# The crossbar's merges two steps later, A21-A22 taken before the transposes, contiguous merge writes

## The chip, the cores and the metric

The kernel runs on one core of one Trainium2 chip. The metric is device time in microseconds, the median of several executions. The engines are PE (matrix products, with PEld for its weight loads), DVE (vector), ACT (scalar: copies and activation functions), POOL (here it issues the accumulating DMAs) and SP (here it issues most of the DMAs). Each engine works through its own queue in order, and waits where an operand is not ready.

## What is computed

A trunk of two layers on x of 512 tokens by 1024 features. Each layer adds half a SwiGLU network, a token mixer, and half a second SwiGLU network; the first layer's mixer is a gated linear recurrence, the second's a spatial gating unit over chunks of 128 tokens. The part that the change touches is the SwiGLU network, which occurs four times with a hidden width of 2816:

```
def swiglu(x, w_in, w_out):
    g, u = jnp.split(x @ w_in, 2, axis=-1)
    return (jax.nn.silu(g) * u) @ w_out

for i in range(DEPTH):
    h = h + 0.5 * swiglu(rms_norm(h, ffn1_norm[i]), ffn1_w_in[i], ffn1_w_out[i])
    ...
    h = h + 0.5 * swiglu(rms_norm(h, ffn2_norm[i]), ffn2_w_in[i], ffn2_w_out[i])
return rms_norm(h, final_norm)
```

Everything is fp32 in and out.

## The kernel before

**Products.** An fp32 factor is split into a high part (`hi`, `whi`: a rounded copy, made by ACT) and a low part (`lo`, `wlo`: the difference, made by DVE), and a product is three matmuls, hi x hi, hi x lo and lo x hi (L423 to L425). On top of that, products of large blocks go by a scheme with seven products in place of eight of a 2 x 2 block product (`seven`). Its left factors are A11, A12, A22 and the sums S1 = A21 - A22, S2 = S1 - A11, S4 = S2 + A12, S3 = -S2 - A22; here A11 and A12 are the left and right half of the features for the first 256 tokens, A21 and A22 those of the last 256 tokens. The products are called P1, P2, P5, P6, P3, P7 and Q4, in this order, on A11, A12, S1, S2, S4, S3 and A22 (`ORDER`, `LEFT`). The right factors are blocks of weights, loaded by SP into buffers `raw`, some of them added to on the way by POOL's accumulating DMAs, some added by DVE (`raw<-raw,raw`).

**One SwiGLU network** (`ffn`) goes through the hidden width in three parts: a pair of 128-column tiles and a chunk of four, then twice a chunk of four and a chunk of four. Each part makes the hidden tiles of its two pieces (`pair_plain` or `chunk`), and then multiplies them by their rows of the output weights (`out_blocks`). In a chunk the products go to PSUM banks A, B and C, ACT and DVE copy and combine them into SBUF tiles `c`, and the gated hidden tiles come out after P3 (tokens 0 to 255, half 0) and after Q4 (tokens 256 to 511, half 1).

**Transposing the hidden tiles.** The output product needs them with features on partitions. For the second piece of each part PE transposes them (L268, tile `e`), one step after they are made. For the first piece (`whole=True`; the pair in one part of three, a chunk of four in the others) it is done by the DMA crossbar, which moves 16-bit elements: `Group.cross` has ACT separate the high and low 16 bits of each fp32 element into planes (`pl`), SP issue the crossbar transposes of the planes (`dt`), and ACT merge the two transposed planes into fp32 again (`merge`). There are twelve such first pieces, each with two halves and two merges to a half. Then `parts` splits a block into hi and lo, and `sums` makes S2, S4 and S3 on DVE.

**Order.** All instructions stand in an order written out by hand. The program runs through a list of steps; a step is one weight block of one product (12 matmuls in a chunk), and a chunk has 14 steps. At step i the loop (L1629 on) runs the hooks `pre`, splits the weights up to step i + 3, runs the hooks `mid` and `rest`, issues loads into buffers that came free, then issues the step's matmuls, and runs the hooks `end` and `late`. `hook(n, phase, fn)` puts work at step n. In `cross` at step n, before: planes at n `mid`, transposes at n `rest`, the two merges at n + 3 and n + 4 (L328), the parts of A11 and A12 at n + 5 and n + 6 (L330), or for half 1 S1's subtraction and its parts at n + 5 (L332, L333), and S2, S4 and S3 from n + 6 (L763). The call follows a chunk's P3 or Q4 by one step, a pair's by two. Small tiles come from a pool of 60 slots.

Of the kernel before, what the change touches and what calls it, by code (L numbers as in the profile page):

```python
# [10 lines left out]
U16 = mybir.dt.uint16  # L11
AF = mybir.ActivationFunctionType
ALU = mybir.AluOpType

P = 128
D = 1024
T = 512
# [36 lines left out]
def trunk(ctx: ExitStack, tc: tile.TileContext, a: dict, out: bass.AP):  # L54
    nc = tc.nc
    PS = bass.MemoryType.PSUM
    cp = ctx.enter_context(tc.tile_pool(name="cp", bufs=1))
    sp = ctx.enter_context(tc.tile_pool(name="sp", bufs=SLOTS))
# [9 lines left out]
    def nm(s):  # L68
        uid[0] += 1
        return f"{s}_{uid[0]}"  # L70
# [16 lines left out]
    def tt(o, x, y, op):  # L87
        nc.vector.tensor_tensor(out=o, in0=x, in1=y, op=op)  # L88
# [7 lines left out]
    def act(o, x, f, **k):  # L96
        nc.scalar.activation(out=o, in_=x, func=f, **k)  # L97
# [118 lines left out]
    def hook(n, phase, fn):  # L216


        hooks.setdefault((n, phase), []).append(fn)
# [29 lines left out]
    class Group:  # L249
# [45 lines left out]
            for c, g in cs:  # L295
                stt(lo[:, c], ps[:, c], g, f32(hi[:, c]), ALU.mult, ALU.subtract)

        def cross(self, n, names, tiles):

            w, pl, dt = 4 * self.n * P, [], {}  # L300

            def planes():
                for h in tiles:
                    t = sp.tile([P, 2 * T], U16, tag="s", name=nm("pl"))[:, :w]
                    act(t.rearrange("p (k b f) -> p k b f", k=2, b=2),
                        h.bitcast(U16).rearrange("p (k f b) -> p k b f", k=2, b=2), AF.Copy)
                    pl.append(t)
                tiles.clear()

            def move():  # L310
                for name, k in names:
                    d = dt[name] = sp.tile([P, 2 * T], U16, tag="s", name=nm("dt"))[:, :w]
                    v = d.rearrange("p (m s t) -> p m s t", s=2, t=P)
                    for s, t in enumerate(pl):
                        nc.sync.dma_start_transpose(out=v[:, :, s, :], in_=t[:, k * w // 2 : (k + 1) * w // 2])
                pl.clear()

            def merge(name):
                t = self.new("S1" if name == "A21" else name)
                act(t.bitcast(U16).rearrange("p (x b) -> p b x", b=2), dt.pop(name).rearrange("p (b x) -> p b x", b=2), AF.Copy)  # L320

            def s1():
                tt(self.f["S1"], self.f["S1"], self.f["A22"], ALU.subtract)
# [12 lines left out]

# [467 lines left out]
    def chunk(w_in, f0, nt, group, opening=None, whole=False):  # L804
# [47 lines left out]
    def pair_plain(w_in, f0, group, first=False):  # L852
# [819 lines left out]
```

## Time and profile before

| | |
|---|---|
| time, median of 3 runs | 1595.22 us (1595.11 to 1600.31) |
| the profiled execution's own time | 1601.47 us |
| its span, first to last instruction | 1599.8 us |
| granted clock of TensorE, mean | 0.999 |
| crossbar transposes (SP) | 96, 3.8 us from issue to landing (median; 2.3 to 8.4) |
| merges (ACT) | 48: 32 of 128x1024 and 16 of 128x512 16-bit elements |
| plane copies (ACT) | 48: 32 of 128x1024 and 16 of 128x512 |
| DMA moved | 289.79 MB, mean 181 GB/s |

How to read the rows: a row of waits names an engine, what it was to write and the helper's line, then who ended the wait, the total in us, the times, and the longest. A row of a timeline has the start in us, the duration in us, the engine, line, operation, what it writes `<-` what it reads, the shapes, and in brackets the idle time of the engine just before it and what ended that. L97, L88 and L94 are the helpers through which all ACT and DVE work goes, so that the tile names tell what an instruction is. A row of a group by shape ends with the count, the busy time in us and the mean duration in ns, and the idle time before them.

### The profile page before, as it was taken

To read this page: it belongs to the slowest core of one execution; us is meant where nothing else is said; L and a number is where in the kernel's file an instruction comes from. 1 tells how busy PE (TensorE), PEld (TensorE's weight loads), DVE (VectorE), ACT (ScalarE), POOL (GpSimd) and SP (SyncE) were. 2 spreads that over 40 slices of the span, in tenths; PEclk is the share of its full clock that TensorE was granted. 3 is DMA by queue.
4 is the path that set the end of the run, shared out by engine and by line. 5 is a ranking of instruction groups with operands and counts; after the bars stand their busy time and mean duration, and the time that the engine had idled before them with its cause. 6 is when DMAs were issued, how large, how long until landed. Compare 5 with 4: busy or idle time off the path is not lost.

```text
span 1599.8 us, 20767 instructions
## 1 busy us (share of the span) xinstructions
PE 1585.2 (99%) x7293; PEld 1314.5 (82%) x7293; DVE 1368.5 (86%) x1834; ACT 1098.4 (69%) x1567; POOL 223.1 (14%) x201
## 2 busy tenths in 40 slices
PE   9999999999999999999999999999999999999998
PEld 7778888898888888888788888888888888888886
DVE  6898897888998897877888978878978988889788
ACT  7757657668777657557677576576886875675676
POOL 2111111100010111111102111111211011111120
PEclk9999999999999999999999999999999999999999
DMA  8779978853294788978838788778878657796793
GB/s 287 175 170 185 226 168 193 213 150 103 82 215 104 175 189 196 220 173 174 213 112 185 177 192 213 178 179 215 226 196 207 158 127 196 179 221 173 173 223 104
DMA packets 208297, 289.79 MB, mean 181 GB/s; under 512 B 55505, under 2 KB 81217, under 8 KB 208193
## 3 DMA queue, kind: packets, MB, share of 16 engines
q1 hardware_dynamic: 158688, 195.33, 40.0%
q0 software_dynamic: 47712, 91.30, 34.4%
q10 hardware_dynamic: 1792, 1.84, 0.4%
q8 instruction: 57, 0.93, 0.2%
q14 instruction: 48, 0.39, 0.1%
HBM read 275.84 MB, written 2.10 MB: 174 GB/s over the span
## 4 chain that ended last, share of the span: by engine, by line
PE 90%; DMA 4%; DVE 3%; issue 1%; ACT 1%; SPq 0%; POOL 0%; ACTq 0%; DVEq 0%; POOLq 0%
PE A L425 13%; PE A L424 13%; PE A L423 13%; PE C L424 7%; PE C L425 7%; PE C L423 7%; PE p L870 4%; PE B L425 4%; PE B L424 4%; PE B L423 4%; PE e L268 2%; PE r L226 2%; PE r L228 2%; PE r L227 2%; DMA raw<-in_ffn_w_in_dram 2%; DMA dt<-pl 1%
## 5 line engine op out<-in xcount | busy, mean ns | idle before, releaser
L88 DVE TENSOR_TENSOR wlo<-raw,whi 128x1024 fp32r<-128x1024 f32 (+1 forms) x537 | 639.2, 1194 | 170.9 <-ACT whi L97 164.6
L97 ACT ACTIVATE whi<-raw 128x1024 fp32r<-128x1024 f32 (+1 forms) x537 | 553.7, 1034 | 324.6 <-PE A L424 81.1
L423 PE MATMUL A<-whi,hi 128*128 128x512 f32 x1016 | 399.0, 393 | 0.8 <-ACT c L97 0.8
L425 PE MATMUL A<-wlo,hi 128*128 128x512 f32 x1016 | 396.0, 390 | 0.0
L424 PE MATMUL A<-whi,lo 128*128 128x512 f32 x1016 | 395.8, 390 | 0.0
L425 PEld LDWEIGHTS A<-wlo,hi 128*128 128x128 f32 x1016 | 190.7, 188 | 40.1 <-DVE wlo L88 0.4
L423 PEld LDWEIGHTS A<-whi,hi 128*128 128x128 f32 x1016 | 190.9, 188 | 39.6 <-ACT c L97 1.2
L424 PEld LDWEIGHTS A<-whi,lo 128*128 128x128 f32 x1016 | 190.9, 188 | 38.8 <-DVE lo L88 0.3
L424 PE MATMUL C<-whi,lo 128*128 128x512 f32 x560 | 218.8, 391 | 1.2 <-DVE lo L88 1.2
L423 PE MATMUL C<-whi,hi 128*128 128x512 f32 x560 | 219.1, 391 | 0.7 <-ACT hi L97 0.7
L425 PE MATMUL C<-wlo,hi 128*128 128x512 f32 x560 | 218.7, 390 | 0.0
L139 POOL DMA_DIRECT2D raw<-in_ffn_w_in_dram x82 | 99.1, 1216 | 718.2 <-DMA raw<-in_ffn_w_out_dram 302.6
L139 POOL DMA_DIRECT2D raw<-in_ffn_w_out_dram x72 | 83.3, 1196 | 376.5 <-DVE wlo L88 152.4
L88 DVE TENSOR_TENSOR raw<-raw,raw 128x1024 f32<-128x1024 f32 x108 | 129.8, 1202 | 0.5
L88 DVE TENSOR_TENSOR lo<-a,hi 128x512 fp32r<-128x512 f32 (+1 forms) x188 | 123.0, 662 | 2.9 <-ACT hi L97 2.8
L424 PEld LDWEIGHTS C<-whi,lo 128*128 128x128 f32 x560 | 105.5, 188 | 23.9 <-DVE lo L88 2.0
L97 ACT ACTIVATE hi<-a 128x512 fp32r<-128x512 f32 (+1 forms) x188 | 111.9, 600 | 18.8 <-DVE a L88 16.6
L423 PEld LDWEIGHTS C<-whi,hi 128*128 128x128 f32 x560 | 105.4, 188 | 23.1 <-ACT hi L97 1.1
L425 PEld LDWEIGHTS C<-wlo,hi 128*128 128x128 f32 x560 | 105.6, 188 | 21.9
L424 PE MATMUL B<-whi,lo 128*128 128x512 f32 x280 | 109.1, 390 | 0.1
L423 PE MATMUL B<-whi,hi 128*128 128x512 f32 x280 | 109.1, 390 | 0.0
L425 PE MATMUL B<-wlo,hi 128*128 128x512 f32 x280 | 109.0, 389 | 0.0
(183 smaller groups left out, 2102.7 us busy)
## 6 DMA issues: line engine op xcount, KB each, us to landing
raw<-in_ffn_w_in_dram SPq DMA_DIRECT2D x161, 512.0 KB, 4.5
raw<-in_ffn_w_out_dram SPq DMA_DIRECT2D x100, 512.0 KB, 5.0
raw<-in_ffn_w_in_dram POOLq DMA_DIRECT2D x82, 512.0 KB, 6.7
raw<-in_ffn_w_out_dram POOLq DMA_DIRECT2D x60, 512.0 KB, 7.8
raw<-in_sg_w_in_dram SPq DMA_DIRECT2D x20, 512.0 KB, 6.7
raw<-in_ffn_w_in_dram SPq DMA_DIRECT2D x34, 256.0 KB, 5.1
raw<-in_rec_w_in_dram SPq DMA_DIRECT2D x16, 512.0 KB, 3.9
raw<-in_sg_w_in_dram POOLq DMA_DIRECT2D x12, 512.0 KB, 8.4
```

The costliest lines, as they stand in the source:

```text
L88: nc.vector.tensor_tensor(out=o, in0=x, in1=y, op=op)
L97: nc.scalar.activation(out=o, in_=x, func=f, **k)
L139: nc.gpsimd.dma_start(out=self.v, in_=src, accum_op=ALU.add)
L226: nc.tensor.matmul(ps, wh, xh, start=start, stop=False)
L227: nc.tensor.matmul(ps, wh, xl, start=False, stop=False)
L228: nc.tensor.matmul(ps, wl, xh, start=False, stop=stop)
L268: nc.tensor.transpose(ps[:, o : o + P], src(q, s), ident)
L423: nc.tensor.matmul(ps, zh, wh, start=fresh and i == 0, stop=False, **k)
L424: nc.tensor.matmul(ps, zl, wh, start=False, stop=False, **k)
L425: nc.tensor.matmul(ps, zh, wl, start=False, stop=end, **k)
L870: nc.tensor.matmul(bank_of(half, s), z, (sub.lo if m == 2 else sub.hi)[:, q, :], start=left[2] == "2" and (h, q, m) == (0, 0, 0), stop=lef ...
```

## The change

**Timing.** The merges go from steps n + 3 and n + 4 to n + 5 and n + 6, the parts of the left blocks from n + 5 and n + 6 to n + 7 and n + 8, and S2, S4 and S3 from n + 6, n + 7 and n + 8 to n + 8, n + 9 and n + 10.

**A21 - A22.** Before, A22 and A21 were transposed, A21 was merged into S1's tile, and DVE subtracted A22 from it. Now DVE subtracts the right half from the left half of each token tile of half 1, in place, before the planes are made; the left half that goes through the crossbar is S1 itself. One subtraction per half 1 is replaced by two of half the width.

**Planes and merges.** The planes are copied by halves of the features, four copies in place of two for each half of the tokens, each followed by its transpose. The merge runs over the elements with the two planes as its inner loop: it writes contiguously and reads from the two planes in turn. Before it ran over one plane after the other, reading contiguously and writing every second 16-bit element.

```
-            hook(n, "mid", planes)
-            hook(n, "rest", move)
-            for i, (name, _) in enumerate(names):
-                hook(n + 3 + i, "mid", lambda name=name: merge(name))
-                if name in ("A11", "A12"):
-                    hook(n + 5 + i, "mid", lambda name=name: self.parts(name))
-            if names[-1][0] == "A21":
-                hook(n + 5, "pre", s1)
-                hook(n + 5, "mid", lambda: self.parts("S1"))
+            def move():
+                pl = [sp.tile([P, 2 * T], U16, tag="s", name=nm("pl"))[:, : 2 * w] for _ in tiles]
+                for k, name in enumerate(names):
+                    c = slice(k * w, (k + 1) * w)
+                    d = dt[name] = sp.tile([P, 2 * T], U16, tag="s", name=nm("dt"))[:, : 2 * w]
+                    v = d.rearrange("p (m s t) -> p m s t", s=2, t=P)
+                    for s, (t, h) in enumerate(zip(pl, tiles)):
+                        act(t[:, c].rearrange("p (b f) -> p b f", b=2),
+                            h.bitcast(U16)[:, c].rearrange("p (f b) -> p b f", b=2), AF.Copy)
+                        nc.sync.dma_start_transpose(out=v[:, :, s, :], in_=t[:, c])
                 tiles.clear()
...
             def merge(name):
-                t = self.new("S1" if name == "A21" else name)
-                act(t.bitcast(U16).rearrange("p (x b) -> p b x", b=2), dt.pop(name).rearrange("p (b x) -> p b x", b=2), AF.Copy)
+                act(self.new(name).bitcast(U16).rearrange("p (x b) -> p x b", b=2),
+                    dt.pop(name).rearrange("p (b x) -> p x b", b=2), AF.Copy)
...
         if whole:
-            g.cross(n, (("A22", 1), ("A21", 0)) if half else (("A11", 0), ("A12", 1)),
-                    [tiles.pop(2 * half + s) for s in range(2)])
+            hs = [tiles[2 * half + s] for s in range(2)]
             if half:
-                sums(g, n + 6)
+                for h in hs:
+                    tt(h[:, : g.n * P], h[:, : g.n * P], h[:, g.n * P :], ALU.subtract)
+                sums(g, n + 8)
+            g.cross(half, hs, (n, "mid"), ((n + 5, "mid"), (n + 6, "mid")), [(n + 7, "mid"), (n + 8, "mid")][: 2 - half])
             return
```

The instructions of PE, SP and POOL and their order stay as they were, but for names and which half of the features a transpose carries first. What moves stands on ACT and DVE.

ACT in the third part of the first layer's second network (near 740 us), where the first chunk's blocks are merged while the second chunk is multiplied. Before:

```order
L97 ACTIVATE whi_6803<-raw_6450 128x1024
L97 ACTIVATE hi_6807<-a_1446_6748 128x512
L97 ACTIVATE whi_6826<-raw_6428 128x1024
L97 ACTIVATE a_1468_6831<-dt_6754 128x2x512
L97 ACTIVATE whi_6847<-raw_6450 128x1024
L97 ACTIVATE s_1471_6852<-dt_6757 128x2x512
L97 ACTIVATE c_1458_6792<-c_1458_6792,rt_4669 128x512
L97 ACTIVATE c_1459_6800<-c_1459_6800,rt_4669 128x512
L97 ACTIVATE whi_6871<-raw_6632 128x1024
L97 ACTIVATE hi_6875<-s_1471_6852 128x512
```

The same place on ACT, after:

```order
L97 ACTIVATE a_1459_6832<-dt_6686 128x1024
L97 ACTIVATE whi_6849<-raw_6453 128x1024
L97 ACTIVATE hi_6854<-a_1454_6809 128x512
L97 ACTIVATE whi_6872<-raw_6475 128x1024
L97 ACTIVATE hi_6877<-a_1459_6832 128x512
L97 ACTIVATE c_1455_6817<-c_1455_6817,rt_4684 128x512
L97 ACTIVATE c_1456_6825<-c_1456_6825,rt_4684 128x512
L97 ACTIVATE whi_6897<-raw_6657 128x1024
L97 ACTIVATE s_1474_6901<-dt_6777 128x1024
L97 ACTIVATE c_1476_6911<-C_6883 128x512
L97 ACTIVATE c_1477_6919<-C_6884 128x512
L97 ACTIVATE whi_6921<-raw_6691 128x1024
```

The merges of half 1 (A22 and S1 before, S1 first after) have moved behind two more weight splits, and where they stood there are now the hi parts of A11 and A12.

DVE at the same place, up to the gating of the second chunk (`c<-c,rt,c`), whose tiles PE then transposes. Before:

```order
L88 TENSOR_TENSOR wlo_6848<-raw_6450,whi_6847 128x1024
L88 TENSOR_TENSOR s_1471_6852<-s_1471_6852,a_1468_6831 128x512
L88 TENSOR_TENSOR wlo_6872<-raw_6632,whi_6871 128x1024
L88 TENSOR_TENSOR lo_6876<-s_1471_6852,hi_6875 128x512
L88 TENSOR_TENSOR a_1440_6720<-s_1471_6852,a_1440_6720 128x512
L88 TENSOR_TENSOR wlo_6899<-raw_6664,whi_6898 128x1024
L88 TENSOR_TENSOR a_1446_6748<-a_1440_6720,a_1446_6748 128x512
L88 TENSOR_TENSOR wlo_6918<-raw_6592,whi_6917 128x1024
L94 SCALAR_TENSOR_TENSOR s_1471_6852<-a_1440_6720,a_1468_6831 128x512
L88 TENSOR_TENSOR wlo_6941<-raw_6614,whi_6940 128x1024
L88 TENSOR_TENSOR wlo_6960<-raw_6428,whi_6959 128x1024
L88 TENSOR_TENSOR c_1487_6929<-C_6856,c_1487_6929 128x512
```

The same place on DVE, after:

```order
L88 TENSOR_TENSOR wlo_6922<-raw_6691,whi_6921 128x1024
L88 TENSOR_TENSOR wlo_6942<-raw_6617,whi_6941 128x1024
L88 TENSOR_TENSOR lo_6946<-s_1474_6901,hi_6945 128x512
L88 TENSOR_TENSOR a_1454_6809<-s_1474_6901,a_1454_6809 128x512
L88 TENSOR_TENSOR wlo_6969<-raw_6639,whi_6968 128x1024
L88 TENSOR_TENSOR a_1459_6832<-a_1454_6809,a_1459_6832 128x512
L88 TENSOR_TENSOR wlo_6989<-raw_6453,whi_6988 128x1024
L88 TENSOR_TENSOR c_1487_6957<-C_6883,c_1487_6957 128x512
L94 SCALAR_TENSOR_TENSOR c_1487_6957<-c_1487_6957,rt_4684,c_1455_6817 128x512
L88 TENSOR_TENSOR c_1488_6965<-C_6884,c_1488_6965 128x512
L94 SCALAR_TENSOR_TENSOR c_1488_6965<-c_1488_6965,rt_4684,c_1456_6825 128x512
L94 SCALAR_TENSOR_TENSOR s_1474_6901<-a_1454_6809,a_1480_6925 128x512
```

S1's subtraction is gone, S1's lo part and the sums S2 and S4 (`a<-s,a`, `a<-a,a`) stand two weight splits nearer to the gating, and S3 (`s<-a,a`) behind it.

ACT in the opening (near 58 us), where the pair's half 0 is merged and the copies `c<-A` free bank A for PE. Before:

```order
L97 ACTIVATE whi_637<-raw_279 128x1024
L97 ACTIVATE hi_641<-s_89_427 128x512
L97 ACTIVATE a_143_645<-dt_536 128x2x256
L97 ACTIVATE pl_647<-h_588 128x512
L97 ACTIVATE pl_649<-h_592 128x512
L97 ACTIVATE c_149_665<-A_161 128x512
L97 ACTIVATE c_150_673<-A_162 128x512
L97 ACTIVATE whi_675<-raw_307 128x1024
L97 ACTIVATE hi_679<-a_137_621 128x256
```

The same place on ACT, after:

```order
L97 ACTIVATE whi_639<-raw_279 128x1024
L97 ACTIVATE hi_643<-s_89_427 128x512
L97 ACTIVATE pl_647<-h_590 128x256
L97 ACTIVATE pl_648<-h_594 128x256
L97 ACTIVATE pl_647<-h_590 128x256
L97 ACTIVATE pl_648<-h_594 128x256
L97 ACTIVATE c_147_667<-A_161 128x512
L97 ACTIVATE c_148_675<-A_162 128x512
L97 ACTIVATE whi_677<-raw_307 128x1024
L97 ACTIVATE a_151_681<-dt_531 128x512
L97 ACTIVATE whi_698<-raw_159 128x1024
L97 ACTIVATE a_155_702<-dt_536 128x512
```

The merge that stood ahead of the plane copies and of the copies from bank A has moved behind them.

More of the change, by code (lines that the diff above doesn't have):

```diff
@@ L296, in direct @@
                 stt(lo[:, c], ps[:, c], g, f32(hi[:, c]), ALU.mult, ALU.subtract)
[L298 to L307, printed above, removed]
-                tiles.clear()
[L310 to L316, printed above, removed]
-            def merge(name):
-                t = self.new("S1" if name == "A21" else name)
-                act(t.bitcast(U16).rearrange("p (x b) -> p b x", b=2), dt.pop(name).rearrange("p (b x) -> p b x", b=2), AF.Copy)
-            def s1():
-                tt(self.f["S1"], self.f["S1"], self.f["A22"], ALU.subtract)
-            hook(n, "mid", planes)
-            hook(n, "rest", move)
-            for i, (name, _) in enumerate(names):
-                hook(n + 3 + i, "mid", lambda name=name: merge(name))
-                if name in ("A11", "A12"):
-                    hook(n + 5 + i, "mid", lambda name=name: self.parts(name))
-            if names[-1][0] == "A21":
-                hook(n + 5, "pre", s1)
-                hook(n + 5, "mid", lambda: self.parts("S1"))
@@ new lines, in cross @@
+        def cross(self, half, tiles, planes, merges, parts):
+            w, names = 2 * self.n * P, ("A12", "A11") if half == 0 else ("S1", "A22")
+            if half == 0:
+                names = names[::-1]
+            dt = {}
+            def move():
[8 more added lines that the diff above has]
+                        nc.sync.dma_start_transpose(out=v[:, :, s, :], in_=t[:, c])
+                tiles.clear()
+            def merge(name):
+                act(self.new(name).bitcast(U16).rearrange("p (x b) -> p x b", b=2),
+                    dt.pop(name).rearrange("p (b x) -> p x b", b=2), AF.Copy)
+            hook(*planes, move)
+            for name, at in zip(names, merges):
+                hook(*at, lambda name=name: merge(name))
+            for name, at in zip(names, parts):
+                hook(*at, lambda name=name: self.parts(name))
```

## The prediction

> **What bounds the kernel now.** I read the page's busy shares first, then the waits of PE by stretches, then ACT's waits on the crossbar, and last the rows around single PE waits.
>
> ```profile
> PE 1585.2 (99%) x7293; PEld 1314.5 (82%) x7293; DVE 1368.5 (86%) x1834; ACT 1098.4 (69%) x1567; POOL 223.1 (14%) x201
> ```
>
> PE is busy in all but 14.6 us of the 1599.8 us span. The change leaves PE's instructions and their order alone, so it wins or loses only in PE's waits. Of the next rows the first four are the waits of PE between 40 and 92 us (the opening), the last is all of them after 92 us:
>
> ```profile
> PE e L268 <- DVE c L94: 1.5, 3, 1.1
> PE C L424 <- DVE lo L88: 1.2, 1, 1.2
> PE A L423 <- ACT c L97: 0.8, 1, 0.8
> PE C L423 <- ACT hi L97: 0.7, 1, 0.7
> ...
> PE e L268 <- DVE c L94: 2.5, 5, 1.0
> ```
>
> One such wait in PE's timeline:
>
> ```profile
> 289.35 0.39 PE L423 MATMUL A<-whi,hi 128*128 128x512 f32 x1
> 289.57 0.39 PE L424 MATMUL A<-whi,lo 128*128 128x512 f32 x1
> ...
> 292.07 0.27 PE L268 MATMUL e<-ident,c 128*128 128x128 f32 x1
> 292.84 0.98 PE L268 MATMUL e<-ident,c 128*128 128x128 f32 x7 [0.50 <-DVE c L94]
> ```
>
> Matmuls start 0.22 to 0.23 us apart but are drawn 0.39 long, so each recorded wait costs about 0.16 us more than it shows. After 92 us that makes 2.5 + 5 x 0.16 = 3.3 us. In the opening it is 1.0 us for bank A, 1.5 + 0.5 = 2.0 us for the transposes, and 1.9 + 0.3 = 2.2 us for bank C at the first output block, where the clock then falls:
>
> ```profile
> 85.00:90.00 5.00, 4.10 (x11) 0.66 0.35 61
> ```
>
> The columns are PE's busy time and matmuls, the granted clock, and DMA. A third of the clock for 5 us is 1.7 us. All that this change could touch is thus 3.3 + 1.0 + 2.0 + 2.2 + 1.7 = 10.2 us.
>
> Where these waits come from. ACT waits for the crossbar's transposes 13 times, 24.6 us in all:
>
> ```profile
> ACT a L97 <- DMA dt<-pl: 20.4, 9, 3.6
> ACT s L97 <- DMA dt<-pl: 4.2, 4, 1.9
> ```
>
> The place with the longest PE wait after 92 us, ACT and then DVE:
>
> ```profile
> 744.16 1.37 ACT L97 ACTIVATE a<-dt 128x1024 uint16<-128x1024 uint16 x1 [3.43 <-DMA dt<-pl]
> 747.74 1.36 ACT L97 ACTIVATE s<-dt 128x1024 uint16<-128x1024 uint16 x1 [1.31 <-DMA dt<-pl]
> ...
> 746.46 1.23 DVE L88 TENSOR_TENSOR wlo<-raw,whi 128x1024 fp32r<-128x1024 f32 x1 [1.68 <-ACT whi L97]
> 749.14 0.70 DVE L88 TENSOR_TENSOR s<-s,a 128x512 f32<-128x512 f32 x1 [1.45 <-ACT s L97]
> 751.27 1.23 DVE L88 TENSOR_TENSOR wlo<-raw,whi 128x1024 fp32r<-128x1024 f32 x1 [1.44 <-PE A L425]
> ...
> 756.58 0.68 DVE L94 SCALAR_TENSOR_TENSOR s<-a,a 128x512 f32<-128x512 f32 x1
> 757.18 2.35 DVE L88 TENSOR_TENSOR wlo<-raw,whi 128x1024 fp32r<-128x1024 f32 x2
> 759.45 0.69 DVE L88 TENSOR_TENSOR c<-C,c 128x512 f32<-128x512 f32 x1
> ...
> 761.56 0.75 DVE L94 SCALAR_TENSOR_TENSOR c<-c,rt,c 128x512 f32<-128x512 f32 x1
> 762.37 0.99 PE L268 MATMUL e<-ident,c 128*128 128x128 f32 x7 [1.00 <-DVE c L94]
> ```
>
> Two merges hold ACT 3.43 + 1.31 = 4.7 us, the weight splits behind them come late, DVE stands idle 1.68 + 1.45 + 1.44 = 4.6 us, then runs without a gap from 751.27 to 762.3 and hands the gated tile c to PE's transposes late. The opening, in the same order of cause:
>
> ```profile
> 57.74 0.79 ACT L97 ACTIVATE a<-dt 128x512 uint16<-128x512 uint16 x1 [1.52 <-DMA dt<-pl]
> 60.05 0.50 PE L423 MATMUL A<-whi,hi 128*128 128x512 f32 x1 [0.82 <-ACT c L97]
> 61.47 1.23 DVE L88 TENSOR_TENSOR wlo<-raw,whi 128x1024 fp32r<-128x1024 f32 x1 [3.60 <-ACT whi L97]
> 67.33 0.98 PE L268 MATMUL e<-ident,c 128*128 128x128 f32 x7 [1.06 <-DVE c L94]
> 79.39 1.06 ACT L97 ACTIVATE whi<-raw 128x1024 fp32r<-128x1024 f32 x1 [4.14 <-DMA raw<-in_ffn_w_out_dram]
> ```
>
> The merge at 57.74 delays the plane copies, the copies that free bank A, and through whi the DVE. The row at 79.39 is another matter: there a weight block is late.
>
> **The change part by part.** Prices of one instruction, from the groups by shape (busy in total, mean ns):
>
> ```profile
> L97 ACT ACTIVATE a<-dt 128x1024 uint16<-128x1024 uint16 x24 | 32.9, 1372 | 19.0 <-DMA dt<-pl 18.8
> L97 ACT ACTIVATE pl<-c 128x1024 uint16<-128x1024 uint16 x32 | 32.9, 1054 | 2.7 <-DVE c L94 2.6
> L97 ACT ACTIVATE a<-dt 128x512 uint16<-128x512 uint16 x12 | 9.3, 777 | 1.5 <-DMA dt<-pl 1.5
> L97 ACT ACTIVATE pl<-h 128x512 uint16<-128x512 uint16 x16 | 9.0, 612 | 0.0
> L88 DVE TENSOR_TENSOR a<-y,h 128x256 f32<-128x256 f32 x16 | 5.8, 422 | 0.0
> L88 DVE TENSOR_TENSOR s<-s,a 128x512 f32<-128x512 f32 x8 | 5.5, 693 | 5.3 <-ACT s L97 5.2
> ```
>
> *Merges two steps later.* A chunk's step is 12 matmuls, 12 x 0.227 = 2.7 us, so each merge gets 5.4 us more; the longest wait is 3.6 us. All 13 waits should go. At the place above ACT is free 4.7 us earlier, against a PE wait of 1.25 + 0.32 = 1.6 us. What is late next there: DVE's work before c. It loses S1's subtraction and the sum s<-a,a (0.69 us each, the latter now behind c), and the halves' lo parts move two steps towards c but stay inside DVE's former idle time. I let all 3.3 us after 92 us go. In the opening the 1.52 us wait goes against PE's 1.0 us for bank A, and DVE's 3.60 us against 1.5 of the 2.0 us of transposes: 2.5 us. The wait for bank C and the clock stay, because the weight block at 79.39 is bound by its transfer: 0.
>
> *Parts and sums behind them.* In the opening the sum a<-a,a of 128x256 now stands before s<-e,a, which feeds bank C's wait. That is one 0.42 us at most, and I count it in full: +0.4 us. Elsewhere the sums S4 and S3 are needed only in the output block, after the rest of the second chunk.
>
> *A21-A22 on token tiles.* Twelve subtractions leave DVE (8 of 0.69, 4 of about 0.42 us). There come 16 of 128x256 (0.42 each) and 8 of 128x128, which no row shows: between half of 0.42 and 0.42. Together DVE changes by -7.2 + 6.8 + 1.7 to 3.4, at most +3 us over twelve places. They stand right behind the last gating of a chunk, and the plane copies on ACT, the transposes on SP, the weight loads behind these on SP, and PE through whi now wait up to 0.84 us longer there. The merge that stood ahead of the plane copies (1.37 us) has moved away, which pays for that: 0.
>
> *Planes by half, merges written contiguously.* 64 copies of 128x512 and 32 of 128x256 replace 32 and 16 of twice the size. By busy time (9.0 / 16 = 0.56 against 32.9 / 32 = 1.03) a pair costs 0.1 us more per large copy, and the small ones lie between 0.28 and 0.56 each: +3 to +12 us on ACT in all. A merge that reads both planes in turn is in no row. Below stands the plane copy, which also writes contiguously (1054 ns); above I take twice the present merge (2744 ns), since each element may be fetched alone. I take the near one, 1054: 32 x 0.32 + 16 x 0.165 = -12.9 us on ACT. ACT is busy 69%, so 0.8 us of each step are free, and this is worth 0 on the path.
>
> [...] The rows say that stepping by two elements on the write side (1372) costs more than on the read side (1054). [...]
>
> *Queues.* SP's and POOL's instructions keep their order; only the transposes of half 1 carry the left half first. 96 transposes as before: 0.
>
> **The sum.** -3.3 - 2.5 + 0.4 = -5.4 us against the profiled execution, 1601.5 to 1596.1. The median of the runs, 1595.2, is 6.3 us below the profiled one, and some of that may be these very waits being shorter. If all of it came out of the 10.2 us in proportion, 0.38 x 5.4 = 2.1 us are left to gain; if none, 5.4. I take the middle, 3.7: 1591.5 us.
>
> **The rivals.**
> - *The opening loosens too.* Everything up to the second plane copies runs 2.5 us earlier, so the weight loads behind the transposes on SP do as well, bank C's wait (2.2) and the clock's fall (1.7) go. For it: the loads stand behind the transposes. Against it: PE arrives earlier by the same 2.5 us. All 10.2 us then: about 1585.
> - *Nothing to gain.* The change does not do what it says: in the median runs the transposes land in time and the merges hardly wait, or the sums and lo parts moved towards c fill DVE as its idle time did. For it: the 6.3 us between profile and median. Then 1594 to 1597.
> - *Slower: the merge that reads in turn.* If it takes t instead of 1.37 us, two merges in two successive steps have 1.37 + 0.84 = 2.2 us each before ACT runs over; there it decides. At 2.7 us each of the 32 large ones overruns by 0.5: 17 us at most, 11 us if the three-step lead of the splits swallows a third, some 1606. Against it: the plane copy's steps cost nothing visible. [...]
>
> **How the numbers follow.** First case 0.65, with its own range 1589.5 to 1594; the opening loosens 0.06; nothing to gain 0.18; slow merges 0.11, of which 0.03 stay within the bound. A measurement of this kernel tells about 0.5% from no change, 8 us: below 1587.2 is faster, above 1603.2 slower. Faster is the loosened opening and a tail of the first case, 0.07; slower 0.08; the rest, 0.85, lies between. The range from 1586.5 to 1600 leaves out most of the loosened opening and of the slow merges, 0.14 together, and holds the 1600.3 us that one run of the kernel before took.
>
> **What would show it.** Right: ACT's waits on dt<-pl at most 2 us in all; PE's waits on c after 92 us under 0.8 us; bank A's wait near 60 us gone; merges of 128x1024 near 1.05 us. Wrong: merges over 2.2 us with DVE waiting for whi behind them; new waits of PE on whi or wlo in the second chunk; DVE without a gap before c as now; bank C's wait grown by more than 0.4 us.

## The result and the profile after

| | before | after |
|---|---|---|
| median of 12 runs each | 1597.82 us (1595.11 to 1602.51) | 1596.55 us (1594.33 to 1597.82) |
| ratio after / before | | 0.9990, 95% interval 0.9981 to 0.9999 |
| the profiled execution's own time | 1601.47 us | 1596.20 us |
| its span | 1599.8 us | 1594.5 us |

The time is 1.3 us lower, less than a measurement of this kernel tells from no change by the prediction's bound of 0.5%. Between the two profiled executions the difference is 5.3 us, close to the 5.4 of the forecast sum, but what makes it up is different, and most of it does not show in the medians. By the starts of the same matmuls in the two traces, about 3.7 us are gained in the opening and 3.6 us later, and 2.0 us are lost.

The busy shares, after:

```profile
PE 1584.9 (99%) x7293; PEld 1313.9 (82%) x7293; DVE 1370.3 (86%) x1846; ACT 1099.0 (69%) x1615; POOL 222.2 (14%) x201
```

PE is as busy as before; what can differ is its waits and its granted clock. All of PE's waits from 40 us to the end, after (the products' lines L423 to L425 are L415 to L417 now):

```profile
PE C L416 <- DVE lo L88: 1.2, 1, 1.2
PE C L415 <- ACT hi L97: 0.5, 1, 0.5
```

The waits for the gated tile `c` and the one for bank A near 60 us are gone. On ACT no wait for a transpose (`dt<-pl`) is left of the 24.6 us. Bank C's wait at the first output block is still there, and so is the fall of the clock behind it. The windows of the opening, after (PE busy and matmuls, PEld, DVE, ACT, POOL, granted clock, DMA share, GB/s):

```profile
80.00:85.00 5.00, 3.28 (x10) 2.38 (x10) 5.00 (x9) 3.14 (x5) 0.00 (x0) 0.82 0.50 110
85.00:90.00 5.00, 5.00 (x20) 4.07 (x19) 5.00 (x11) 2.52 (x4) 2.10 (x2) 0.84 0.50 86
```

The groups by shape, after (count, busy us, mean ns, idle before):

```profile
L97 ACT ACTIVATE pl<-c 128x512 uint16<-128x512 uint16 x64 | 36.0, 622 | 7.7 <-DVE c L94 6.0 <-DVE c L88 1.7
...
L97 ACT ACTIVATE a<-dt 128x1024 uint16<-128x1024 uint16 x24 | 28.1, 1172 | 0.0
L97 ACT ACTIVATE pl<-h 128x256 uint16<-128x256 uint16 x32 | 10.6, 403 | 0.0
...
L88 DVE TENSOR_TENSOR h<-h 128x128 f32<-128x128 f32 x8 | 1.9, 282 | 0.0
```

A merge of 128x1024 takes 1172 ns in place of 1372, and the subtraction of 128x128, which no row of before shows, 282 ns. The plane copies now wait for DVE 7.7 us in all, where it was 2.7.

One new wait stands in no list of waits, because it is hardly longer than the 0.16 us by which a matmul is drawn too long; it shows in the starts. ACT and then PE near 136 us, where a chunk of four is about to go through the crossbar, after:

```profile
131.31 1.06 ACT L97 ACTIVATE whi<-raw 128x1024 fp32r<-128x1024 f32 x1 [1.66 <-PE C L416]
132.40 0.63 ACT L97 ACTIVATE pl<-c 128x512 uint16<-128x512 uint16 x1
133.79 1.68 ACT L97 ACTIVATE pl<-c 128x512 uint16<-128x512 uint16 x3 [0.76 <-DVE c L94]
...
136.32 1.26 ACT L97 ACTIVATE c<-A 128x512 f32<-128x512 f32 x2
...
136.32 0.39 PE L416 MATMUL A<-whi,lo 128*128 128x512 f32 x1
136.55 0.39 PE L417 MATMUL A<-wlo,hi 128*128 128x512 f32 x1
136.95 0.50 PE L415 MATMUL A<-whi,hi 128*128 128x512 f32 x1
137.28 0.40 PE L416 MATMUL A<-whi,lo 128*128 128x512 f32 x1
```

The same place on ACT, before:

```profile
134.97 1.06 ACT L97 ACTIVATE whi<-raw 128x1024 fp32r<-128x1024 f32 x1 [1.66 <-PE C L424]
136.07 1.06 ACT L97 ACTIVATE pl<-c 128x1024 uint16<-128x1024 uint16 x1
137.45 1.06 ACT L97 ACTIVATE pl<-c 128x1024 uint16<-128x1024 uint16 x1 [0.33 <-DVE c L94]
...
139.37 0.58 ACT L97 ACTIVATE c<-A 128x512 f32<-128x512 f32 x1
```

Read from the `whi` in the first row of each, the copy that frees bank A starts 5.01 us later in the kernel after (136.32 - 131.31) and 4.40 us later in the kernel before (139.37 - 134.97), a difference of 0.6 us. With copies by halves the first is the left half of token tile 0, the second already needs token tile 1, which DVE finishes later, so ACT waits 0.76 us with half of tile 0 uncopied. PE's matmuls, 0.227 us apart elsewhere, start 0.40 and 0.33 us apart here. That is 0.3 us at this place, about 0.2 us at the mean of eight (near 137, 253, 604, 721, 931, 1047, 1387 and 1504 us), and 1.7 us in all.

### The profile page after: what moved, and what is told of

It is laid out like the page before. It is cut to its first block, busy times and chain, and to the rows that moved or that the text cites. A ratio compares the mean times of both kernels' runs of the same rounds, so it can differ in the third digit from the quotient of the medians.

```text
span 1594.5 us, 20905 instructions
## 1 busy us (share of the span) xinstructions
PE 1584.9 (99%) x7293; PEld 1313.9 (82%) x7293; DVE 1370.3 (86%) x1846; ACT 1099.0 (69%) x1615; POOL 222.2 (14%) x201
## 4 chain that ended last, share of the span: by engine, by line
PE 94%; DMA 3%; DVE 1%; issue 0%; ACT 0%; SPq 0%; POOL 0%; POOLq 0%; ACTq 0%; DVEq 0%
PE A L415 14%; PE A L416 14%; PE A L417 14%; PE C L416 8%; PE C L417 8%; PE C L415 8%; PE p L864 4%; PE B L416 4%; PE B L417 4%; PE B L415 4%; PE e L268 2%; DMA raw<-in_ffn_w_in_dram 2%; PE r L226 2%; PE r L228 2%; PE r L227 2%; PE Q L415 1%
## 5 line engine op out<-in xcount | busy, mean ns | idle before, releaser
L415 PE MATMUL A<-whi,hi 128*128 128x512 f32 x1016 | 399.6, 393 | 0.0
L417 PE MATMUL A<-wlo,hi 128*128 128x512 f32 x1016 | 395.8, 390 | 0.0
L415 PEld LDWEIGHTS A<-whi,hi 128*128 128x128 f32 x1016 | 190.8, 188 | 41.2 <-ACT c L97 2.9
L417 PEld LDWEIGHTS A<-wlo,hi 128*128 128x128 f32 x1016 | 190.7, 188 | 40.1 <-DVE wlo L88 0.4
L415 PE MATMUL C<-whi,hi 128*128 128x512 f32 x560 | 218.9, 391 | 0.5 <-ACT hi L97 0.5
L417 PE MATMUL C<-wlo,hi 128*128 128x512 f32 x560 | 218.7, 391 | 0.0
L415 PEld LDWEIGHTS C<-whi,hi 128*128 128x128 f32 x560 | 105.5, 188 | 23.0 <-ACT hi L97 1.0
L417 PEld LDWEIGHTS C<-wlo,hi 128*128 128x128 f32 x560 | 105.4, 188 | 21.8
L415 PE MATMUL B<-whi,hi 128*128 128x512 f32 x280 | 109.0, 389 | 0.0
L417 PE MATMUL B<-wlo,hi 128*128 128x512 f32 x280 | 108.9, 389 | 0.0
```

The lines of the kernel that those rows point to most:

```text
L415: nc.tensor.matmul(ps, zh, wh, start=fresh and i == 0, stop=False, **k)
L417: nc.tensor.matmul(ps, zh, wl, start=False, stop=end, **k)
```

## The experiments

Three chips were used, and each kernel is compared with runs of the kernel before on its own chip. Medians in us:

| kernel | chip | before, runs | this, runs | ratio, 95% interval |
|---|---|---|---|---|
| before again | 1 | 1597.15, 30 | 1599.21, 12 | 1.0006 [0.9996, 1.0016] |
| after again | 1 | 1597.15, 30 | 1596.74, 12 | 0.9989 [0.9978, 0.9999] |
| times only | 1 | 1597.15, 30 | 1592.40, 7 | 0.9965 [0.9952, 0.9978] |
| after, whole planes | 1 | 1597.15, 30 | 1594.09, 12 | 0.9975 [0.9966, 0.9985] |
| times + planes by half | 2 | 1598.95, 21 | 1594.59, 10 | 0.9975 [0.9965, 0.9985] |
| times + contiguous merges | 2 | 1598.95, 21 | 1592.95, 8 | 0.9965 [0.9953, 0.9977] |
| times + token tiles | 2 | 1598.95, 21 | 1594.17, 10 | 0.9973 [0.9962, 0.9983] |
| times + other order in the opening | 2 | 1598.95, 21 | 1593.13, 6 | 0.9965 [0.9951, 0.9978] |
| times only, again | 3 | 1599.28, 17 | 1592.78, 5 | 0.9965 [0.9952, 0.9978] |
| one step later in place of two | 3 | 1599.28, 17 | 1595.38, 12 | 0.9985 [0.9973, 0.9997] |
| times + token tiles but in the opening | 3 | 1599.28, 17 | 1593.85, 5 | 0.9967 [0.9955, 0.9979] |
| times + contiguous merges + other order | 3 | 1599.28, 17 | 1593.22, 5 | 0.9963 [0.9951, 0.9975] |

### The kernel before, once more

No edit. How large are its waits in another execution?

> The kernel before, unchanged, for a second profile. Theory (the waits that the merges cause vary from run to run, and the profile on record caught many): 1596 to 1599 us, ratio 1.000; in this profile PE's waits on c and on bank A after 92 us are again there but sum to another value than 2.5 us recorded, between 0.5 and 2.5. Rival (the profile on record is the usual case and the rest of the 6 us lay elsewhere): the same 2.3 to 2.7 us recorded, at the same places.

PE's waits in the opening and then after 92 us, and ACT's for the transposes:

```profile
PE e L268 <- DVE c L94: 1.1, 2, 0.9
PE C L424 <- DVE lo L88: 0.7, 1, 0.7
...
PE e L268 <- DVE c L94: 4.6, 6, 1.0
PE C L423 <- ACT c L97: 0.6, 1, 0.6
...
ACT a L97 <- DMA dt<-pl: 22.0, 9, 5.8
ACT s L97 <- DMA dt<-pl: 4.6, 5, 2.3
```

Neither expectation met it. The waits do vary, but here they are larger: 5.2 us recorded after 92 us in place of 2.5, behind ACT waits of 26.6 us in place of 24.6. The clock did not fall in the opening (granted 1.00 in both windows from 80 to 100 us). So the waits of the prediction's profiled execution were no exception, but both profiled executions (1601.47 and 1600.00 us) are among the longer ones: the 30 runs on this chip have a median of 1597.15, from 1594.85 to 1602.83. The median of three runs, 1595.22, was low.

### The kernel after, once more

No edit.

> The changed kernel, unchanged, beside the others on one chip. Theory: 1595.5 to 1597.5 us, ratio 0.998 to 1.000, no PE wait on c after 92 us, eight small PE waits on bank A (about 0.2 us each beyond the pitch), bank C's wait of 2.1 us and the slow clock in the opening as before. Rival (the eight waits are chance): they are gone or lie elsewhere.

1596.74 us, and the same picture: eight waits on bank A, none on `c`, none of ACT on `dt`, and bank C's wait with the fall of the clock (granted 0.83 from 80 to 90 us). Bank C's two waits are 2.7 us recorded here, where the first execution had 1.7.

### The later times alone

The kernel before with only the step numbers of the change:

```
-                hook(n + 3 + i, "mid", lambda name=name: merge(name))
+                hook(n + 5 + i, "mid", lambda name=name: merge(name))
...
-                    hook(n + 5 + i, "mid", lambda name=name: self.parts(name))
+                    hook(n + 7 + i, "mid", lambda name=name: self.parts(name))
...
-                hook(n + 5, "pre", s1)
-                hook(n + 5, "mid", lambda: self.parts("S1"))
+                hook(n + 7, "pre", s1)
+                hook(n + 7, "mid", lambda: self.parts("S1"))
...
-                sums(g, n + 6)
+                sums(g, n + 8)
```

> The kernel before with only the times moved: merges, parts, S1's subtraction and sums two steps later; planes, subtraction and merge writes as before. Theory (later merges are the whole gain, and copying the planes by half costs 1.6 us of it): 1594 to 1595.5 us, ratio about 0.998, no waits of ACT on the transposes and none of PE on c after 92 us, no wait on bank A. Rival (the other two parts contribute to the gain): no faster than the changed kernel, 1596.5 us or more.

1592.40 us, 4.75 below before, better than expected, and steady: 1591.60 to 1593.94. All the waits of PE in the whole program:

```profile
PE warm L1510 <- DVE warm L1505: 1.3, 1, 1.3
PE C L424 <- DVE lo L88: 1.2, 1, 1.2
PE C L423 <- ACT hi L97: 0.3, 1, 0.3
```

The difference closes. The second execution of before has 1.8 us in three waits from 40 to 92 us and 5.2 us in seven later; with 0.16 us for each wait that is 8.6 us. Here it is 1.5 us in two, 1.8 with the same. The 6.8 us between them stand against a difference of 7.6 us in these two executions' times (1600.00 and 1592.40). The rest of the change, then, takes back 1596.74 - 1592.40 = 4.3 us of the 4.75.

### The change with whole planes

The kernel after, with each token tile's planes copied at once as before:

```
                 pl = [sp.tile([P, 2 * T], U16, tag="s", name=nm("pl"))[:, : 2 * w] for _ in tiles]
+                for t, h in zip(pl, tiles):
+                    act(t.rearrange("p (k b f) -> p k b f", k=2, b=2),
+                        h.bitcast(U16).rearrange("p (k f b) -> p k b f", k=2, b=2), AF.Copy)
                 for k, name in enumerate(names):
...
-                        act(t[:, c].rearrange("p (b f) -> p b f", b=2),
-                            h.bitcast(U16)[:, c].rearrange("p (f b) -> p b f", b=2), AF.Copy)
                         nc.sync.dma_start_transpose(out=v[:, :, s, :], in_=t[:, c])
```

> The changed kernel, but each token tile's planes copied at once (two copies to a half of the tokens, as before). Theory: the eight waits on bank A go, 1.6 us less than the changed kernel, 1594 to 1595.5 us. Rival (those waits come from the merges' new place or are covered elsewhere): within 0.5 us of the changed kernel.

1594.09 us, 2.65 below after on the same chip. The eight waits on bank A are gone (1.7 us), and 3 of the 12 runs have the lower mean clock of 0.998 in place of 6 of 12. The planes by half are the dearest of the three additions. What is left, 1.7 us above the later times alone on the same chip, falls to the token tiles and the contiguous merges together.

### The later times with planes by half

On the later times alone, the plane copies in the order of the change, half by half:

```
-                for h in tiles:
-                    t = sp.tile([P, 2 * T], U16, tag="s", name=nm("pl"))[:, :w]
-                    act(t.rearrange("p (k b f) -> p k b f", k=2, b=2),
-                        h.bitcast(U16).rearrange("p (k f b) -> p k b f", k=2, b=2), AF.Copy)
-                    pl.append(t)
+                pl.extend(sp.tile([P, 2 * T], U16, tag="s", name=nm("pl"))[:, :w] for _ in tiles)
+                for name, k in names:
+                    c = slice(k * w // 2, (k + 1) * w // 2)
+                    for t, h in zip(pl, tiles):
+                        act(t[:, c].rearrange("p (b f) -> p b f", b=2),
+                            h.bitcast(U16)[:, c].rearrange("p (f b) -> p b f", b=2), AF.Copy)
```

> The kernel with only the times moved (1592.4 us), and the planes copied by halves of the features as in the change. Theory (the second copy waits for the second token tile on DVE, and the copies from bank A stand behind it): eight PE waits on bank A of about 0.2 us, 1.6 us in all, 1593.5 to 1595 us. Rival (those waits belong to the subtraction on token tiles): no such waits, 1592.0 to 1592.9 us.

The waits are back. PE near 134 us, and ACT's wait for DVE in the plane copies:

```profile
134.07 0.39 PE L426 MATMUL A<-wlo,hi 128*128 128x512 f32 x1
134.47 0.50 PE L424 MATMUL A<-whi,hi 128*128 128x512 f32 x1
134.81 0.40 PE L425 MATMUL A<-whi,lo 128*128 128x512 f32 x1
...
ACT pl L97 <- DVE c L94: 6.1, 8, 0.8
```

1594.59 us, 1.6 above the next kernel, which ran on the same chip with contiguous merges and without the halves. Token tiles are absent here, so the halves alone make these waits.

### The later times with contiguous merges

```
-                act(t.bitcast(U16).rearrange("p (x b) -> p b x", b=2), dt.pop(name).rearrange("p (b x) -> p b x", b=2), AF.Copy)
+                act(t.bitcast(U16).rearrange("p (x b) -> p x b", b=2), dt.pop(name).rearrange("p (b x) -> p x b", b=2), AF.Copy)
```

> Only the times moved, and the merges written contiguously, reading the two planes in turn. Theory: a merge of 128x1024 takes 1.17 in place of 1.37 us, nobody waits for it, 1591.8 to 1592.9 us. Rival (shorter merges free ACT where PE waits for it, bank C in the opening): 0.5 us or more faster, under 1591.8.

1592.95 us, at the upper end of what was expected, and the ratio of the later times alone, 0.9965. A faster merge is worth nothing here, where no wait on a merge is left.

### The later times with A21 - A22 on token tiles

Planes stay whole here:

```
-                t = self.new("S1" if name == "A21" else name)
+                t = self.new(name)
...
-            def s1():
-                tt(self.f["S1"], self.f["S1"], self.f["A22"], ALU.subtract)
...
-            if names[-1][0] == "A21":
-                hook(n + 7, "pre", s1)
+            if names[-1][0] == "S1":
...
-            g.cross(n, (("A22", 1), ("A21", 0)) if half else (("A11", 0), ("A12", 1)),
-                    [tiles.pop(2 * half + s) for s in range(2)])
+            hs = [tiles.pop(2 * half + s) for s in range(2)]
+            if half:
+                for h in hs:
+                    tt(h[:, : g.n * P], h[:, : g.n * P], h[:, g.n * P :], ALU.subtract)
+            g.cross(n, (("A22", 1), ("S1", 0)) if half else (("A11", 0), ("A12", 1)), hs)
```

> Only the times moved, and A21-A22 taken on the token tiles, planes of a token tile copied at once. Theory: ACT waits longer for the planes of half 1 (about 0.4 us each), nobody on PE's side feels it, 1592.0 to 1593.2 us. Rival (this part costs the 1.7 us by which the changed kernel with whole planes is slower than the times alone): 1593.5 to 1594.5 us, with the clock falling in the opening in some runs.

1594.17 us, 1.2 above the kernel with contiguous merges and within what the rival gave. Only part of it can be placed, since the profiled execution (1592.76 us) is the fastest of the ten. PE's recorded waits after 40 us are no larger in sum than in the later times alone, but one on `c` is new:

```profile
PE C L420 <- DVE lo L88: 1.2, 1, 1.2
PE e L268 <- DVE c L94: 0.3, 1, 0.3
```

It stands near 287 us. Near 1148 us two matmuls on bank A start 0.37 and 0.34 us behind the one before in place of 0.227, which the later times alone do not have. The two places make about 0.6 us. Three of its ten runs have the lower mean clock of 0.998, near 1595.3 us.

### Another order in the opening

The prediction put bank C's wait and the clock's fall down to a transfer. Here no transfer changes; the late weight block is split a step later, so that the products ahead of it get their parts first:

```
-    ahead = {0: 0, 1: 2, 2: 3, 3: 4, 4: 6, 5: 7}
+    ahead = {0: 0, 1: 2, 2: 3, 3: 4, 4: 6, 5: 7, 23: 25}
...
-                hook(n + 1 + lag, "mid", lambda: self.parts("S1" if first else name))
+                hook(n + 1 + lag, "pre" if first and n == 23 else "mid", lambda: self.parts("S1" if first else name))
```

> Only the times moved, and in the opening the second chunk's block A22 and S1 with its parts put ahead of the split of the late weight block on ACT and DVE; no transfer is changed. Theory as put before the result (bank C waits because a weight block's transfer is late): the wait stays at 2 us, 1591.9 to 1592.9 us. Rival (it waits because S1 stands behind that block's split in the queues of ACT and DVE, and the block itself comes in time): the wait on bank C goes or falls below 0.5 us, the clock does not fall there, 1589.9 to 1590.9 us.

PE's waits between 40 and 92 us:

```profile
PE A L424 <- DVE lo L88: 1.1, 1, 1.1
PE C L423 <- ACT whi L97: 0.6, 1, 0.6
```

Neither expectation met it. The two waits of the output block have gone from their place, so the transfer alone was not their cause: the ready parts stood behind the late block in ACT's queue. But as much comes back elsewhere, at bank A and at a weight split of bank C (recorded 1.7 us against 1.5), and the time is 1593.13, no better. In this execution ACT waits for no weight transfer from 60 to 93 us (in the later times alone twice, 2.1 us in all), and DVE is busy for 4.97 and 5.00 us of the two windows of 5 us from 80 to 90 us (5.00 and 5.00 in the later times alone). That speaks for DVE's queue as what is left to bind PE there; no run tests it. All six runs lie between 1592.97 and 1593.57.

### The later times alone, on a third chip

No edit to the later times alone.

> Only the times moved, again, beside the next three. Every theory: ratio to the kernel before 0.9955 to 0.9975, no wait of ACT on the transposes, none of PE on c after 92 us.

0.9965 once more. Its median is 6.5 us below that of before on this chip.

### One step later

Merges at n + 4, parts at n + 6, sums from n + 7, halfway to the change:

```
-                hook(n + 3 + i, "mid", lambda name=name: merge(name))
+                hook(n + 4 + i, "mid", lambda name=name: merge(name))
...
-                    hook(n + 5 + i, "mid", lambda name=name: self.parts(name))
+                    hook(n + 6 + i, "mid", lambda name=name: self.parts(name))
...
-                hook(n + 5, "pre", s1)
-                hook(n + 5, "mid", lambda: self.parts("S1"))
+                hook(n + 6, "pre", s1)
+                hook(n + 6, "mid", lambda: self.parts("S1"))
...
-                sums(g, n + 6)
+                sums(g, n + 7)
```

> Everything moved by one step in place of two. Theory (a step is 2.7 us, the waits of ACT on the transposes were up to 3.6 to 5.8 us): most waits of ACT go, some of 1 to 3 us stay, PE's waits on c after 92 us fall below 0.5 us recorded, within 1 us of the times moved by two. Rival (two steps are needed): 1.5 us or more above them.

1595.38 us, 2.6 above two steps, as the rival had it. ACT's waits have nearly gone, and yet PE waits for `c` as in the kernel before. ACT's wait, PE's after 92 us, and then ACT, DVE and PE ahead of one such wait:

```profile
ACT a L97 <- DMA dt<-pl: 5.0, 2, 2.7
...
PE e L268 <- DVE c L94: 5.2, 6, 1.0
...
258.26 1.38 ACT L97 ACTIVATE a<-dt 128x1024 uint16<-128x1024 uint16 x1
259.48 1.99 ACT L97 ACTIVATE pl<-c 128x1024 uint16<-128x1024 uint16 x2
261.36 1.05 ACT L97 ACTIVATE whi<-raw 128x1024 fp32r<-128x1024 f32 x1
...
277.39 1.23 DVE L88 TENSOR_TENSOR wlo<-raw,whi 128x1024 fp32r<-128x1024 f32 x1 [1.17 <-ACT whi L97]
...
283.81 0.69 DVE L94 SCALAR_TENSOR_TENSOR s<-a,a 128x512 f32<-128x512 f32 x1
284.42 1.22 DVE L88 TENSOR_TENSOR wlo<-raw,whi 128x1024 fp32r<-128x1024 f32 x1
...
287.66 0.75 DVE L94 SCALAR_TENSOR_TENSOR c<-c,rt,c 128x512 f32<-128x512 f32 x1
...
286.21 0.39 PE L425 MATMUL A<-wlo,hi 128*128 128x512 f32 x1
...
288.47 0.77 PE L268 MATMUL e<-ident,c 128*128 128x128 f32 x5 [1.00 <-DVE c L94]
```

The same place with two steps (the later times, third chip):

```profile
258.81 2.00 ACT L97 ACTIVATE pl<-c 128x1024 uint16<-128x1024 uint16 x2
260.70 1.05 ACT L97 ACTIVATE whi<-raw 128x1024 fp32r<-128x1024 f32 x1
...
275.69 1.22 DVE L88 TENSOR_TENSOR wlo<-raw,whi 128x1024 fp32r<-128x1024 f32 x1 [1.41 <-ACT whi L97]
...
286.40 0.75 DVE L94 SCALAR_TENSOR_TENSOR c<-c,rt,c 128x512 f32<-128x512 f32 x1
287.07 0.68 DVE L94 SCALAR_TENSOR_TENSOR s<-a,a 128x512 f32<-128x512 f32 x1
...
286.76 0.39 PE L425 MATMUL A<-wlo,hi 128*128 128x512 f32 x1
287.00 1.20 PE L268 MATMUL e<-ident,c 128*128 128x128 f32 x8
```

Both are counted from PE's last product ahead of the transposes, at 286.21 and 286.76 us. The last gating of `c` starts 1.45 us behind it with one step and 0.36 us ahead of it with two, so `c` is 1.8 us later, and at this place ACT waits for no transpose at all. With two steps the sum S3 (`s<-a,a`) has moved behind the gating; with one it still stands ahead of it, which is 0.6 us of the 1.8. The rest comes from further up. With one step the first merge stands ahead of the plane copies on ACT, and the weight split behind them is 1.2 us later; DVE's run of work up to `c` then begins 2.3 us later (8.8 us ahead of the product in place of 11.1). Which of the moved pieces counts for how much no run tells. On this chip the first step brings 3.9 us of the median and the second 2.6. The profiled execution (1600.24 us) is one of the longer of its twelve, and the clock fell in it (granted 0.66 from 970 to 975 us), so it has lost more than the median run.

### Token tiles except in the opening

On the later times alone, as the token tiles above, but with the pair of the opening left as before:

```
+            hs = [tiles.pop(2 * half + s) for s in range(2)]
+            left = "A21"
+            if half and where is not bank:
+                left = "S1"
+                for h in hs:
+                    tt(h[:, : g.n * P], h[:, : g.n * P], h[:, g.n * P :], ALU.subtract)
+            g.cross(n, (("A22", 1), (left, 0)) if half else (("A11", 0), ("A12", 1)), hs)
```

> Times moved and A21-A22 taken on token tiles everywhere but in the opening's pair. If the 1 us that the token tiles cost comes from the opening (bank C's wait and with it the clock): within 0.4 us of the times alone. Rival (from the eight whole chunks, where ACT waits for the subtraction and the plane copies come late): 0.7 to 1.3 us above the times alone.

1593.85 us, 1.1 above the later times alone on the same chip, in the rival's range. But with five runs each the two overlap (1592.02 to 1595.01 against 1592.08 to 1594.77). The two profiled executions are 2.0 us apart (1594.74 against 1592.78), and most of that lies in the opening, in a fall of the clock, although the opening's pair has no subtraction on token tiles here:

```profile
80.00:85.00 5.00, 3.35 (x10) 2.13 (x10) 5.00 (x9) 3.06 (x5) 0.00 (x0) 0.82 0.61 109
85.00:90.00 5.00, 5.00 (x20) 3.99 (x19) 5.00 (x12) 2.61 (x5) 2.10 (x2) 0.84 0.48 73
```

The later times alone have a granted clock of 1.00 in both windows on this chip. Of the token tiles the trace shows one wait on `c`, 0.3 us recorded near 289 us, the one that the kernel with token tiles everywhere has near 287 us. What the subtraction costs beyond that stays open, and so does whether it makes the fall more frequent.

### Contiguous merges and the other order together

On the later times alone, both edits shown above.

> Times moved, merges written contiguously, and the opening's S1 ahead of the late weight block. The earlier runs speak for no more than 0.5 us either way against the times alone: the loss at the first output block goes on as waits for wlo and whi there. Rival (shorter merges and the other order help each other): 0.7 us or more below the times alone.

1593.22 us: the two together bring no more than each. Bank A's 1.1 and bank C's 0.6 us stand there as in the run with the order alone, and the five runs are as narrow (1592.63 to 1593.72).

**The best version** is the later times alone: 0.9965 of before on two chips, against 0.9989 for the whole change on the first.

## Why the prediction was right and where it was wrong

**What bounds the kernel: right.** PE's waits and its granted clock are all that moved, and the 8.6 us of the second execution of before fit the ceiling of 10.2.

**Merges two steps later, -3.3 and -2.5: right in the waits, too small in the median.** ACT's 24.6 us on `dt`, the 2.5 us of PE on `c` and bank A's wait near 60 us are gone, in after and in every kernel with the later times that was profiled, but for 0.3 us on `c` with the token tiles. Alone this brought 4.75 us of the median on one chip and 6.5 on another, not 3.7. The mechanism was half told: the gain was put down to the merges' waits on the transposes. The kernel with one step in place of two has most of those waits gone and is still 2.6 us slower: at the place shown, `c` is 1.8 us late because of where the merges and parts stand in the queues of ACT and DVE, S3 among them with 0.6 us.

**+0.4 us for the sum ahead of bank C's wait: not shown.** The waits there vary from run to run, 1.9 and 0.7 us recorded in two executions of before and 1.7 and 2.7 in two of after, so nothing was added that the runs can tell.

**Bank C's wait and the clock stay: right in the outcome, wrong in the cause.** That the block's transfer binds the wait fell with the other order, in which the wait left its place with no transfer changed. But as much came back at another, so no time was to be had by this edit.

**Planes by half, 0: the step that failed.** It was costed as ACT's busy time, +3 to +12 us against free time in each step. The measured sizes lie near its lower end (36.0 + 10.6 us in place of 32.9 + 9.0, +4.7 us in all), but the cost is not the size: the second of the four copies waits for the second token tile (0.76 us at the place shown), and the copies that free bank A stand behind them on the same queue. That is 1.6 us in one pair of kernels and 2.65 us in another, where fewer runs have the lower mean clock as well; 0 was forecast.

**Token tiles, 0: too low by about 1 us.** The prediction let the merge that moved away pay for up to 0.84 us of later gating. The kernels with it are 1.2 and 1.1 us slower than those without, and 1.7 us together with the contiguous merges. The unknown instruction was within its bounds (282 ns). The traces show about 0.6 us of waits in one run and one wait of 0.3 us recorded in the other; the rest is not explained.

**Merges written contiguously, 0 on the path: right.** They take 1172 ns where 1054 was taken and 2744 was the bound, and give nothing. This is the place of the rival of the slow merge, which is refuted: the merge that reads the two planes in turn is 0.20 us faster than the one that wrote every second element, and 0.12 us above the plane copy. The bound of 2744, twice the merge of before, was the author's estimate, and no run shows it; the merges of 128x512 took 682 ns in place of 777 as well.

**The rival "nothing to gain"** gave 1594 to 1597, and the median of 1596.55 lies there, but for another reason. Its mechanism, merges that hardly wait in the usual run, is refuted by the later times alone. The gain was there and was given back.

**From the profile to the median: wrong.** The 6.3 us between the profiled execution and a median of three were taken, by half, for shorter waits in the usual run. With twelve runs in the same comparison the median of before is 1597.82, so 2.6 of the 6.3 us came from a median of only three; 30, 21 and 17 runs on the other occasions gave 1597.15, 1598.95 and 1599.28. The time of 1596.55 is 5.05 us above the forecast of 1591.5: 2.6 us are this base, and 2.4 are gain that did not come (1.3 in place of 3.7), which the two terms of 0 account for (1.6 to 2.65 and about 1.1 us, against 1.05 us more from the later times). The stated range held the time only because it was wide: the first case's own range, 1589.5 to 1594, did not, and that the loss stayed inside is luck.

## What to carry to other kernels

Where an in-order engine waits for a transfer, move the waiting instruction by the longest wait seen, and then look at what stands ahead of what in the queues: here the second step paid 2.6 us, though the first had taken most of the waits on transfers away, and at the place looked at, merges and sums still stood ahead of the work for the tile that PE waits for. Splitting a copy changes which operand its second piece needs; where that is the one made last, everything queued behind it, a bank's release among it, waits as well (here 0.76 us on ACT, and about 0.2 us of PE at each of eight places), and a list of waits may not show it, because a matmul is drawn longer (0.39 us) than the distance between two starts (0.227): compare the starts. Effects of a few us are measured part by part, since three parts of one change here had -4.75, about +1 and about +2 us, and the whole -0.4 to -1.3.

## What the runs showed of the hardware

**The clock fell behind short pauses, and not always.** At the output block of the opening PE pauses twice. In after it was 1.2 and 0.5 us recorded and the granted clock fell to 0.82 and 0.84 in the two windows shown. With contiguous merges on the later times the second pause was longer:

```profile
PE C L424 <- DVE lo L88: 1.2, 1, 1.2
PE C L423 <- ACT hi L97: 0.9, 1, 0.9
```

and its granted clock was 1.00 in every window of 5 us from 80 to 100 us. Of the 12 runs of after, 7 have a mean clock of 0.998 and average 1597.1 us, 5 have 0.999 and average 1595.5, 1.6 us less. This mean is too coarse to count falls: the profiled execution of before has 0.999, with the fall to 0.66. The windows tell more. In each of the five profiled executions with a fall they lack 1.7 us of full clock in all: 5 x 0.34 in before (85 to 90 us) and with one step (970 to 975 us), 5 x (0.18 + 0.16) in after and with token tiles except in the opening (80 to 90 us), and 5 x (0.05 + 0.29) in after once more (80 to 90 us). Ahead of the four falls in the opening PE's recorded pauses were 0.7 and 1.2 us in before, 0.5 and 1.2 in after and with token tiles except in the opening, and 1.5 and 1.2 in after once more.

**A short wait on a bank cost more than itself.** Behind the late matmul of 136.95 the next starts 0.33 us later in place of 0.227, and with the halves alone it is the same (134.47 to 134.81), so a wait of 0.17 us cost 0.1 us more. At the other seven places of after the late matmul starts 0.32 or 0.33 us behind the one before, and the next 0.33 or 0.34 us behind it.

**16-bit copies on ACT** of 128x1024 take 1054 ns reading every second element, 1172 ns reading two planes in turn, both writing contiguously, and 1372 ns writing every second element: the step on the write side cost 0.32 us more than the one on the read side.
